# Seven products in place of two projections for two more units, four input sums moved ahead, lambda moved into another scaling

## The chip, the cores and the metric

The kernel runs on one core of one Trainium2 chip. A core has five engines with a queue of instructions each: TensorE (PE, matrix products, with PEld for the load of the stationary operand), VectorE (DVE), ScalarE (ACT), GpSimd (POOL) and SyncE (SP, which here only issues transfers). The engines run side by side and wait for each other through semaphores. The metric is the time of one execution on the device in microseconds, as the median of several runs; lower is better.

## The reference

A sequence of 16 meta tokens and 512 tokens of width 1024 goes through a layer norm and one input projection, whose columns are split into ten blocks of 1024. Two attention branches work on them:

```python
proj = jnp.einsum('bld,dn->bln', h, w_in[i])
q_d, k_d, v_d, g_d, q_s, k_s, v_s, g_s, m_d, m_s = jnp.split(proj, IN_OFFSETS, axis=-1)

# differential attention, 8 heads, two score maps per head
p = jax.nn.softmax(s, axis=-1)
a = p[:, :, 0] - lam * p[:, :, 1]
y_d = jnp.einsum('bhqk,bhkd->bhqd', a, v)

# stick-breaking attention, 16 heads
a = jnp.where(before, jnp.exp(jax.nn.log_sigmoid(z) + suffix), 0.0)
```

`lam` is a scalar made from `diff_lambda`. Both branches are gated with SiLU, projected, merged with sigmoid gates, projected once more, added to the input and normalised.

## The kernel before

**Precision.** Products are made of 32-bit operands split in two: a rounded high part and the remainder. A product of weights and input then takes three matmuls: high by high, high by remainder, remainder by high. A half of a weight tile (128 rows x 512 columns, four blocks of 128) gets its high part by a cast on ACT (`hi`, L183) and its remainder by a subtraction on DVE (`lo`, L188). `prep` does this for the half that lies `ahead` = 4 halves further on than the one being multiplied, and asks for more loads (`fetch`, L144 on SP).

**Units.** The attention is worked in 16 units: eight heads of the differential kind (`d`), then eight pairs of heads of the stick-breaking kind (`s`). The text counts them from one; the code's `u` counts from zero. While unit `u` makes its scores, exponentials, transposes and values, PE also projects the keys and values of unit `u + 1`, the queries of unit `u + 2`, and in some units (`GATE_AT`, from the fifth on) a gate. `run` goes through the projections' generators, which yield estimated times, and puts in the steps of the attention when their time has come; for example `(9.2, store_k)` is placed when 9.2 us of projections, by these estimates, have been emitted. Within the attention part this only gives the priorities: a planner orders each engine's queue by its own estimates when the kernel is built. `placed` ties the first instruction of a step on each engine behind the one emitted before it. The start, and all that comes after the attention, keep the written order.

**Keys and values, first form** (`stage_k`, `stage_v`, `proj_pos`, L510). Two projections of 128 columns each. Each goes over two halves of the 528 positions (264 each) and eight blocks of the 1024 inputs, with three matmuls for each block: 48 matmuls of 264 columns, 96 for both. ACT and DVE split the keys in high part and remainder (L635, L636), and `store_k` sends them to the two key tiles by DMA (L643, L644).

**Keys and values, second form** (`stage_kv`, L690). The two weight tiles and the two halves of the inputs and of the positions make a 2 x 2 by 2 x 2 block product, and the kernel makes it with seven block products in place of eight (Strassen's scheme in Winograd's form). Each is 4 blocks x 3 matmuls of 264 columns, 84 in all. It needs:
- four sums of weight blocks; three are made by DMA, which loads one block and adds others to it in memory (`rawk`, accumulating transfers that POOL issues, L146, four for each unit), one by DVE (L169);
- four sums of input blocks, which all units share. `input_sums(k)` makes a quarter of them: a small copy on POOL (L660), four operations on DVE over 264 columns (L662 to L665), a cast on ACT (L667) and a remainder on DVE (L668) over 1056 columns;
- sums of the products, on ACT and DVE (L701 to L712), and at the end the keys' split (L696, L697) and `store_k`, all at the end of the seven products since the second half of the keys comes out of the last.

`SEVEN` is the first unit (from zero) with the second form. It is 5 here, so the sixth unit's keys and values are the first to be made so, during the fifth unit. The four sets of input sums stand in the first four units, one in each, at step 8.0. The ring of buffers for accumulated weights opens with the third unit.

**The scores of the first kind** (`d_scores`). For each block of 128 queries DVE adds a bias and finds the minimum (L834), ACT takes the exponential and its sum (L838), and DVE joins the two maps: reciprocals of the two sums (L842), the second of them times minus lambda (L843), the first map times its reciprocal (L844), and the second times its own plus the first (L845).

Of the kernel before, what the change touches and what calls it, by code (L numbers as in the profile page):

```python
# [35 lines left out]

ORDERED = [mybir.EngineType.PE, mybir.EngineType.DVE, mybir.EngineType.Activation, mybir.EngineType.Pool]
WARM = 14
SEVEN = 5
TD = [(0.85, 11.0, 14.5), (0.95, 13.0, 16.5)]  # L40
GATE_AT = {4: 0, 5: 1, 6: 2, 7: 3, 8: 4, 11: 5, 14: 6}
LO, HI = slice(0, 64), slice(64, 128)
# [3 lines left out]
def hybrid_block_kernel(ctx: ExitStack, tc: tile.TileContext, x, meta, emb_g, emb_b, w_in, b_gate,  # L46
# [175 lines left out]
    def placed(work, engines=ORDERED):  # L222

        ins = nc.cur_bb.bb.instructions
        n = len(ins)
        work()
        for e in engines:
            new = next((i for i in ins[n:] if i.engine == e), None)
            old = next((ins[m] for m in range(n - 1, max(n - 400, 0), -1) if ins[m].engine == e), None)
            if new is not None and old is not None:  # L230
                follow(new, old)
# [349 lines left out]
    with tc.tile_pool(name="att", bufs=1) as ap:  # L581
# [75 lines left out]
        def input_sums(k):  # L657


            g.tensor_copy(hP[k][:, :, :M], hM[:, k:k + 5:4])  # L660
            b11, b12, b21, b22 = [hP[k][:, m, ts(n, H2)] for m in range(2) for n in range(2)]
            v.tensor_tensor(b22, b12, b22, op=ALU.subtract)  # L662
            v.tensor_tensor(b12, b11, b12, op=ALU.subtract)
            v.tensor_tensor(b11, b22, b11, op=ALU.subtract)
            v.tensor_tensor(b21, b11, b21, op=ALU.add)  # L665
            h, l = tS[0][:, k:k + 5:4], pair_of("tl", F32R)
            s.copy(h, hP[k])  # L667
            v.tensor_tensor(l, hP[k], h.bitcast(F32), op=ALU.subtract)  # L668
            tL.append(l)
# [139 lines left out]
        def d_scores(unit, h):  # L809

            A = unit["A"]


            bias = ap.tile([P, L], F32, tag="bias", name="bias", bufs=2)
            if h == 0:
                g.iota(bias, pattern=[[-1, L]], base=400, channel_multiplier=1, allow_small_or_imprecise_dtypes=True)
                g.affine_select(bias, bias, pattern=[[-1, L]], compare_op=ALU.is_ge, fill=1e30, base=400,
                                channel_multiplier=1)
            g.tensor_scalar(bias, biases[-1] if h else bias, 0.5 if h else -0.5, None, op0=ALU.mult)
            biases.append(bias)  # L820
            a = apads[h % 2]
            mn = ap.tile([P, NB, 2, 2], F32, tag="mn", name="mn", bufs=2)
            zs = ap.tile([P, NB, 2], F32, tag="zs", name="zs", bufs=2)
            rz = ap.tile([P, NB, 2], F32, tag="rz", name="rz", bufs=2)
            for i in reversed(range(NB)):
                nk = NKEY[i]
                e = [E[c][:, ZOFF[i]:ZOFF[i] + nk] for c in range(2)]
                for c in range(2):
                    m = mn[:, i, c, :]
                    for n, (ps, k0, use) in enumerate(logits(A[c], K[c], i)):  # L830
                        if n == 1:
                            yield
                        b0 = 384 - P * i + k0
                        v.tensor_tensor_reduce(e[c][:, k0:k0 + use], ps[:, :use], bias[:, b0:b0 + use], -1.0, 3e38,  # L834
                                               ALU.add, ALU.min, m[:, n:n + 1])
                    if nk > 512:
                        v.tensor_tensor(m[:, 0:1], m[:, 0:1], m[:, 1:2], op=ALU.min)
                    s.activation(e[c], e[c], AF.Exp, scale=-1.0, bias=m[:, 0:1], accum_out=zs[:, i, c:c + 1])  # L838
                    if c == 0:
                        yield  # L840
                r = rz[:, i, :]
                v.reciprocal(r, zs[:, i, :])  # L842
                v.tensor_scalar(r[:, 1:2], r[:, 1:2], nlam, None, op0=ALU.mult)  # L843
                v.tensor_scalar(e[0], e[0], r[:, 0:1], None, op0=ALU.mult)  # L844
                v.scalar_tensor_tensor(a[:, AOFF[i]:AOFF[i] + nk], e[1], r[:, 1:2], e[0], op0=ALU.mult, op1=ALU.add)  # L845
                yield

        def d_values(unit, ta):
# [105 lines left out]
        for u, (kind, n) in enumerate(UNITS):  # L954
            unit = units[u]
            if u + 3 == SEVEN:
                pools["rawk"] = ap
            last = u + 1 == len(UNITS)
            proj = [] if last else keys_values(units[u + 1], *UNITS[u + 1])
            if u + 2 < len(UNITS):  # L960
                proj.append(stage_q(units[u + 2], *UNITS[u + 2]))
            steps = pending + [(0.6, lambda unit=unit: values(unit, kind))]
            pending = []
            if u + 1 < SEVEN:
                steps.append((9.2, store_k))
            if u in range(SEVEN - 5, SEVEN - 1):
                if not tS:
                    tS.append(ypool.tile([P, KT, L], F32R, tag="ys", name="tS"))
                steps.append((8.0, lambda k=u + 5 - SEVEN: placed(lambda: input_sums(k))))
            if u in GATE_AT and u < 14:  # L970
                proj.append(raw_gate(GATE_AT[u], kept["r"][GATE_AT[u]]))
            if kind == "d":
                ta = {}
                dt, t0, t1 = TD[u in GATE_AT]
                steps += spread(d_scores(unit, n), 0.0, dt, 10)
                parts = transposed(ta, apads[n % 2])
                steps += [(t0 + 0.7 * m, f) for m, f in enumerate(parts)]
                steps.append((t1, lambda: d_values(unit, ta)))
                pending = [(3.0 if n < 7 else 5.8, lambda unit=unit, n=n: d_norm(unit, n))]
            else:  # L980
                if n == 0:
                    diag.append(ap.tile([P, L], F32, tag="bias", name="diag", bufs=2))
                    g.memset(diag[0], 0.0)
                    g.tensor_copy(diag[0][:, L - P:], ident)
                    g.memset(v3[:, 1], 0.0)
                    for a in apads:
                        for i in range(NB):
                            g.memset(a[:, ds(AOFF[i] + NKEY[i] - 1, 1)], 0.0)
                if last:
                    ydT = [pair_of("ydT", n=S) for k in range(4)]  # L990
                    ydT = [ydT[k % 4][:, k // 4, :] for k in range(8)]
                    ysT = ypool.tile([P, 8, S], F32, tag="ys", name="ysT")
                    ysT = [ysT[:, k, :] for k in range(8)]
                    unit["y"] = ysT[7]

                    def fill_in(y, of):
                        placed(lambda: nc.sync.dma_start(y, of), [mybir.EngineType.SP])

                    fill_in(ydT[7], kept["d"][7])
                    for m, (y, of) in enumerate(((ydT, "gd"), (ysT, "gs"))):  # L1000
                        for j in range(7):
                            steps.append((1.3 + 1.5 * (7 * m + j), lambda o=y[j], x=kept[of][j]: fill_in(o, x)))
                    proj += [gate("d", n, lambda: ydT[7]), merge_gate(0, 0), merge_gate(0, 1), merge_gate(0, 2),
                             gate("s", n, lambda: ysT[7])]
                else:
                    if GATE_AT.get(u) == n:
                        yd = gpool.tile([P, S], F32, tag="sg", name="yd")
                        nc.sync.dma_start(yd, kept["d"][n])
                        proj.append(gate("d", n, lambda yd=yd: yd, kept["gd"][n]))
                    else:  # L1010
                        steps += zip((12.0, 24.0), late_gate(ap, *(kept[x][n] for x in ("d", "r", "gd"))))
                    proj.append(gate("s", n, lambda unit=unit: unit["y"], kept["gs"][n]))
                for c in range(2):
                    ta = {}
                    steps += spread(s_scores(unit, c, n == 0), (2.0 + 4.3 * c) if n == 0 else 4.4 * c, 0.85, 5)
                    parts = transposed(ta, apads[c])
                    times = LAST[c] if last else [7.0 + 6.5 * c + 0.7 * m for m in range(3)] + [10.5 + 6.5 * c]
                    steps += zip(times, parts)
                    steps.append((times[3], lambda c=c, ta=ta: s_values(unit, c, n, ta)))
                if last:  # L1020
                    steps.append((LAST[0][0] - 0.1, lambda: state.update(ends=len(nc.cur_bb.bb.instructions))))
            run(proj, steps)
# [236 lines left out]
```

## Time and profile before

| | |
|---|---|
| median of 3 runs | 712.65 us (712.34 to 713.63) |
| the profiled execution | 712.22 us, of which the span is 710.4 us |
| PE busy | 697.5 us (98%) |
| weight loads busy (PEld) | 636.9 us (90%) |
| DVE busy | 571.8 us (80%) |
| ACT busy | 439.2 us (62%) |
| POOL busy | 125.6 us (18%) |
| DMA | 123.36 MB, mean 174 GB/s |

The profile is that of one execution. Its rows give for each instruction or group the engine, the line of the kernel, what is written and from what, and a duration. The busy time of an engine counts a moment once, even where two instructions overlap. Matmuls are pipelined: one lasts longer than the distance to the next, so that its price on PE is the distance between starts. A row of waits reads "engine and line that waited <- engine and line that released it: us in total, times, longest".

### The profile page before, as it was taken

What the parts mean: (1) busy time and instruction counts of PE and PEld (TensorE: products, weight loads), DVE (VectorE), ACT (ScalarE), POOL (GpSimd) and SP (SyncE); (2) the same over time, 40 slices, a digit from 0 to 9 for tenths busy, and PEclk for the clock granted to TensorE, in tenths of its full rate; (3) what the DMA queues carried; (4) which work ended last, traced back from release to release, by engine and by line L of the source; (5) the groups of instructions that cost most, each with busy time, mean ns of one, the idle gap of its engine ahead of it and who ended that gap; (6) DMA issues with size and microseconds to landing.
All of it is one profiled execution on the core that took longest, in us unless ns stands there. A gap on an engine that the chain in (4) does not pass through costs nothing.

```text
span 710.4 us, 13389 instructions
## 1 busy us (share of the span) xinstructions
PE 697.5 (98%) x4494; PEld 636.9 (90%) x4494; DVE 571.8 (80%) x1265; ACT 439.2 (62%) x1065; POOL 125.6 (18%) x143
## 2 busy tenths in 40 slices
PE   9999999999999999999999999999999999999994
PEld 8999999989999898988989998988889998999884
DVE  6888897878787777988878889976666788788897
ACT  5766676757667587776857777666455546455300
POOL 3214210212222111212123120000012102220002
PEclk9999999999999999999999999999999999999997
DMA  9368754879888876899897976646576748795902
GB/s 293 93 169 164 167 133 125 184 181 183 198 200 184 201 177 164 186 215 214 200 217 174 206 171 175 166 133 197 178 174 112 164 123 182 133 198 170 322 15 104
DMA packets 182182, 123.36 MB, mean 174 GB/s; under 512 B 9009, under 2 KB 165074, under 8 KB 182114
## 3 DMA queue, kind: packets, MB, share of 16 engines
q1 hardware_dynamic: 148130, 102.32, 50.1%
q0 software_dynamic: 33664, 19.14, 21.6%
q10 hardware_dynamic: 320, 1.06, 0.4%
q8 instruction: 35, 0.57, 0.3%
q14 instruction: 33, 0.27, 0.1%
HBM read 91.96 MB, written 9.44 MB: 143 GB/s over the span
## 4 chain that ended last, share of the span: by engine, by line
PE 86%; DVE 6%; DMA 3%; ACT 2%; issue 1%; POOL 1%; SPq 0%; ACTq 0%; DVEq 0%; POOLq 0%
PE q L690 16%; PE ps L496 12%; PE ps L494 12%; PE ps L495 12%; PE q L1065 10%; PE ps L510 7%; PE sc L754 6%; PE t L766 4%; DMA lgb<-in_ln_b_dram 1%; PE bank L385 1%; PE tv L723 1%; DVE hr L1215 1%; DMA xt<-in_x_dram 1%; PE av L922 1%; DMA raw<-in_w_out_dram 1%
## 5 line engine op out<-in xcount | busy, mean ns | idle before, releaser
L188 DVE TENSOR_TENSOR wl<-raw,wh 128x512 fp32r<-128x512 f32 x169 | 115.7, 691 | 43.7 <-ACT wh L183 42.2
L494 PE MATMUL ps<-hTh,wh 128*128 128x512 f32 x368 | 145.0, 394 | 0.0
L495 PE MATMUL ps<-hTl,wh 128*128 128x512 f32 x368 | 144.5, 393 | 0.0
L496 PE MATMUL ps<-hTh,wl 128*128 128x512 f32 x368 | 144.4, 392 | 0.0
L183 ACT CAST wh<-raw 128x512 fp32r<-128x512 f32 x169 | 104.4, 625 | 28.0 <-PE ps L495 15.3
L496 PEld LDWEIGHTS ps<-hTh,wl 128*128 128x128 f32 x368 | 69.2, 188 | 13.9
L495 PEld LDWEIGHTS ps<-hTl,wh 128*128 128x128 f32 x368 | 69.2, 188 | 13.1
L494 PEld LDWEIGHTS ps<-hTh,wh 128*128 128x128 f32 x368 | 69.2, 188 | 12.9
L146 POOL DMA_DIRECT2D rawk<-in_w_in_dram x44 | 60.8, 1642 | 96.9 <-DMA rawk<-in_w_in_dram 58.4
L754 PE MATMUL sc<-k,A 128*128 128x264 f32 (+3 forms) x320 | 65.9, 299 | 0.1
L1065 PE MATMUL q<-gh,wh 128*128 128x256 f32 x224 | 63.5, 283 | 0.2 <-ACT t L1074 0.2
L1065 PE MATMUL q<-gl,wh 128*128 128x256 f32 x224 | 63.4, 283 | 0.0
L1065 PE MATMUL q<-gh,wl 128*128 128x256 f32 x224 | 63.4, 283 | 0.0
L907 DVE TENSOR_TENSOR_SCAN e<-e,diag 128x528 f32<-128x528 f32 (+1 forms) x64 | 53.4, 848 | 7.5 <-ACT e L901 7.3
L754 PEld LDWEIGHTS sc<-k,A 128*128 128x128 f32 x320 | 50.3, 189 | 3.3 <-ACT e L901 0.3
L690 PE MATMUL q<-tS,wh 128*128 128x264 f32 x176 | 50.9, 290 | 0.9 <-DVE low L612 0.9
L690 PE MATMUL q<-tl,wh 128*128 128x264 f32 x176 | 50.2, 286 | 0.0
L690 PE MATMUL q<-tS,wl 128*128 128x264 f32 x176 | 50.2, 286 | 0.0
L510 PE MATMUL ps<-hTh,wh 128*128 128x264 f32 x160 | 46.4, 290 | 0.2 <-ACT k L632 0.2
L933 POOL DMA_DIRECT2D ys<-half x14 | 11.8, 840 | 195.9 <-ACT ys L932 119.2
L510 PE MATMUL ps<-hTh,wl 128*128 128x264 f32 x160 | 45.6, 286 | 0.0
L510 PE MATMUL ps<-hTl,wh 128*128 128x264 f32 x160 | 45.5, 285 | 0.0
(291 smaller groups left out, 1851.4 us busy)
## 6 DMA issues: line engine op xcount, KB each, us to landing
raw<-in_w_in_dram SPq DMA_DIRECT2D x141, 256.0 KB, 3.3
rawk<-in_w_in_dram POOLq DMA_DIRECT2D x44, 256.0 KB, 6.0
rawk<-in_w_in_dram SPq DMA_DIRECT2D x33, 256.0 KB, 3.9
k<-ks SPq DMA_DIRECT2D x60, 132.0 KB, 3.1
raw<-in_w_out_dram SPq DMA_DIRECT2D x16, 256.0 KB, 3.9
k<-ks SPq DMA_DIRECT2D x60, 66.0 KB, 2.8
A<-low SPq DMA_DIRECT2D x28, 128.0 KB, 2.8
raw<-in_w_br_diff_dram SPq DMA_DIRECT2D x12, 256.0 KB, 4.7
```

Source lines behind the costliest of these rows:

```text
L146: second[l] = [lambda raw=raw, x=x: g.dma_start(raw, x, accum_op=ALU.add) for x in more]
L183: s.copy(wh, raw)
L188: eng.tensor_tensor(wl, raw, wh.bitcast(F32), op=ALU.subtract)
L494: pe.matmul(ps, wh[:, k % 4, :], hTh[:, k, M:], start=(k == 0), stop=False)
L495: pe.matmul(ps, wh[:, k % 4, :], hTl[:, k, M:], start=False, stop=False)
L496: pe.matmul(ps, wl[:, k % 4, :], hTh[:, k, M:], start=False, stop=(k == KT - 1))
L510: pe.matmul(ps[:, :H2], a[:, k % 4, :], b[:, k, ts(c, H2)], start=(k == 0 and m == 0), stop=(k == KT - 1 and m == 2))
L690: pe.matmul(bank, a[:, k, :], b, start=start and k == 0 and j == 0, stop=k == 3 and j == 2, skip_group_check=not start)
L754: pe.matmul(ps[:, :n], q, K[:, m, k0:k0 + n], start=(m == 0), stop=(m == 1))
L766: pe.transpose(t[:, o:o + P], a[:, AOFF[i] + j * P:AOFF[i] + (j + 1) * P], ident)
L907: v.tensor_tensor_scan(rev, rev, diag[0][:, L - nk:][:, ::-1], 0.0, ALU.mult, ALU.max)
L1065: pe.matmul(bank, a[:, k, :], b[:, n, k, :], start=start and k == 0 and m == 0, stop=k == 3 and m == 2, skip_group_check=not start)
```

## The change

Three edits.

1. `SEVEN` becomes 3: the keys and values of the fourth and fifth unit, made during the third and the fourth, take the second form too. Their `store_k` at step 9.2 goes, since `stage_kv` stores by itself; the ring for accumulated weights opens with the first unit in place of the third; and the list of loads has seven weight halves for each of these units where it had four.
2. The four sets of input sums stand in the first unit (three, at steps 5.0, 9.0 and 13.0) and in the second (one, at 5.0).
3. In `d_scores`, minus lambda is multiplied in the scaling of the second map, which now comes first, and the first map is scaled in the operation that joins them. The separate product of one column goes.

```diff
-SEVEN = 5
+SEVEN = 3
...
                 r = rz[:, i, :]
                 v.reciprocal(r, zs[:, i, :])
-                v.tensor_scalar(r[:, 1:2], r[:, 1:2], nlam, None, op0=ALU.mult)
-                v.tensor_scalar(e[0], e[0], r[:, 0:1], None, op0=ALU.mult)
-                v.scalar_tensor_tensor(a[:, AOFF[i]:AOFF[i] + nk], e[1], r[:, 1:2], e[0], op0=ALU.mult, op1=ALU.add)
+                v.tensor_scalar(e[1], e[1], r[:, 1:2], nlam, op0=ALU.mult, op1=ALU.mult)
+                v.scalar_tensor_tensor(a[:, AOFF[i]:AOFF[i] + nk], e[0], r[:, 0:1], e[1], op0=ALU.mult, op1=ALU.add)
                 yield
...
             if u + 1 < SEVEN:
                 steps.append((9.2, store_k))
-            if u in range(SEVEN - 5, SEVEN - 1):
+            if u + 1 < SEVEN:
                 if not tS:
                     tS.append(ypool.tile([P, KT, L], F32R, tag="ys", name="tS"))
-                steps.append((8.0, lambda k=u + 5 - SEVEN: placed(lambda: input_sums(k))))
+                steps += [(5.0 + 4.0 * (k % 3), lambda k=k: placed(lambda: input_sums(k))) for k in range(4) if k // 3 == u]
```

## The prediction

> Units are counted from one: the profile's first unit is the loop's u = 0. Each unit's matmuls start with the keys and values of the unit after it.
>
> **What bounds the kernel now.** I read the page's engine totals first, then a table of stretches cut at the first key matmul of each unit (units one to five), then the chain of waits, then who waits for whom.
>
> ```profile
> PE 697.5 (98%) x4494; PEld 636.9 (90%) x4494; DVE 571.8 (80%) x1265; ACT 439.2 (62%) x1065; POOL 125.6 (18%) x143
> ```
>
> ```profile
> core 0: us, PE busy (x) PEld busy (x) DVE busy (x) ACT busy (x) POOL busy (x), PEclk, DMA share, GB/s
> 39.90:59.50 19.60, 19.60 (x142) 18.58 (x141) 17.91 (x55) 13.19 (x37) 4.41 (x5) 1.00 0.61 165
> 59.50:83.50 24.00, 24.00 (x172) 22.82 (x171) 19.97 (x61) 15.97 (x42) 7.46 (x7) 1.00 0.83 159
> 83.50:107.60 24.10, 24.10 (x173) 22.84 (x173) 20.31 (x61) 16.39 (x43) 3.11 (x2) 1.00 0.76 167
> 107.60:131.70 24.10, 24.10 (x173) 22.87 (x172) 20.73 (x62) 16.41 (x43) 3.13 (x2) 1.00 0.56 141
> 131.70:159.80 28.10, 28.10 (x185) 25.83 (x184) 22.83 (x66) 18.95 (x49) 5.51 (x4) 1.00 0.78 177
> ```
>
> PE has no idle time in the units that change, at a granted clock of 1.00: a matmul taken away there ends the kernel earlier by its interval, as long as PE's operands keep coming. The fifth unit already uses seven products, and is longer only by the gate projection that it carries. In the chain of waits:
>
> ```profile
> 97.50 3.03 PE ps L510 x25
> 409.30 2.92 PE q L690 x24
> ```
>
> A matmul over 264 columns takes 3.03 / 25 = 0.121 us, in the two-projection form (L510), and 2.92 / 24 = 0.122 in the seven-product form (L690). The busy time of one (286 ns) is no price, since they overlap. Outside its start PE waits for another engine almost nowhere:
>
> ```profile
> PE q L690 <- DVE low L612: 0.9, 2, 0.6
> ```
>
> DVE is the engine behind. In the first unit it is busy 17.91 of 19.60 us. What it waits for from the first unit to the fourth (39.9 to 131.7 us), longest first:
>
> ```profile
> DVE wl L188 <- ACT wh L183: 5.6, 4, 2.0
> DVE rz L842 <- ACT e L838: 1.8, 2, 0.9
> DVE ax L788 <- PE t L766: 1.7, 3, 0.8
> DVE am L792 <- ACT am L790: 1.0, 2, 0.5
> DVE ks L636 <- ACT ks L635: 0.5, 1, 0.5
> DVE e L834 <- PE sc L754: 0.3, 1, 0.3
> DVE al L772 <- ACT ah L771: 0.3, 1, 0.3
> ```
>
> That is 11.2 us in four units; the first has 0.8 of it (the rows of L636 and L834), the others 10.4, or 3.5 each. This is the room into which the change can put DVE work.
>
> **The change, part by part.** *Matmuls.* In the third and fourth unit, 96 matmuls of 264 columns (two projections, 2 halves x 8 blocks x 3 terms each) become 84 (7 x 4 x 3). 12 fewer in each, 24 x 0.121 = 2.9 us. The table gives the same another way. The gate of the fifth unit is 24 matmuls of 512 columns, here such a run and what follows it:
>
> ```profile
> 154.32 0.40 PE L494 MATMUL ps<-hTh,wh 128*128 128x512 f32 x1
> 159.79 0.28 PE L690 MATMUL q<-hTh,wh 128*128 128x264 f32 x1
> ```
>
> 24 of them lie between the two starts, 5.47 us. 28.10 - 5.47 = 22.63, against 24.10 of the fourth unit: 1.47 less, twice 2.9.
>
> *DVE.* Prices are from start to start, because ends overlap:
>
> ```profile
> 41.53 1.89 DVE L188 TENSOR_TENSOR wl<-raw,wh 128x512 fp32r<-128x512 f32 x3
> 90.82 0.21 DVE L843 TENSOR_SCALAR rz<-rz,nlam 128x1 f32<-128x1 f32 x1
> 90.95 0.57 DVE L844 TENSOR_SCALAR e<-e,rz 128x528 f32<-128x528 f32 x1
> 97.43 0.42 DVE L665 TENSOR_TENSOR hF<-hF 128x264 f32<-128x264 f32 x1
> 97.78 0.42 DVE L834 CUSTOM_DVE_ANT_0 e<-sc,bias 128x272 f32<-128x272 f32 x1
> 100.12 1.26 DVE L668 TENSOR_TENSOR tl<-hF,tS 128x1056 fp32r<-128x1056 f32 x1
> 101.30 0.30 DVE L834 CUSTOM_DVE_ANT_0 e<-sc,bias 128x144 f32<-128x144 f32 x1
> ```
>
> 512 columns cost (1.89 - 0.69) / 2 = 0.60, 264 columns 0.35, a whole remainder of the sums 1.18, the small lambda product 0.13.
> - A unit that turns to seven products adds three weight remainders and one sum of weights (4 x 0.60) and three more operations over 264 columns (five in place of two): 3.45 us. Two units: 6.9.
> - Lambda: the 0.13 goes, four times a unit. The new first scaling reads two scalars per row in place of one; no row has this pair on these shapes. Bounds: nothing, or another 0.13 (the price of a whole extra operation). I take nothing, because the multiplication adds no pass over the columns: -0.5 in each of the eight units of that kind.
> - One set of input sums is 4 x 0.35 + 1.18 = 2.6. None is added: the first unit gets two more (+5.2), the second keeps one, third and fourth lose theirs.
>
> With each moved set go a copy on POOL (L660) and a cast on ACT (L667) into the first unit, ahead of what those queues held there; POOL is busy 4.41 and ACT 13.19 of its 19.60 us, so they find room.
>
> First unit: +5.2 - 0.5 = +4.7 into 0.8 of room, so DVE is up to 3.9 us late at its end. Second: 3.5 of room and 0.5 freed, which takes up that 3.9. Third and fourth: 3.45 - 2.6 - 0.5 = +0.4, and 1.45 less time, into 3.5: 1.7 left in each. The work fits over four units, but not inside the first.
>
> What becomes late is the weights' remainder (L188), which PE's projections read, and the rows of scores. The weights have cover:
>
> ```profile
> 46.72 0.68 DVE L188 TENSOR_TENSOR wl<-raw,wh 128x512 fp32r<-128x512 f32 x1
> 59.74 0.28 PE L510 MATMUL ps<-hTh,wl 128*128 128x264 f32 x1
> ```
>
> The first is the remainder of the first half of the third unit's key weights, the second its first use: 12.3 us of lead. 3.9 fits in that. Scores that come late let projections go ahead of them, because the engines' order around them is written at build. So the price of the moved sums lies between 0 and 3.9; I take 0.3, near the end that the lead points to.
>
> *ACT.* Three more weight casts and one more copy in the third and fourth unit, less one cast of a sum:
>
> ```profile
> L183 ACT CAST wh<-raw 128x512 fp32r<-128x512 f32 x169 | 104.4, 625 | 28.0 <-PE ps L495 15.3
> ```
>
> Four at 0.63 at most are 2.5, on 16.4 of busy time in 22.6 us. Nothing.
>
> *Transfers.* Each of the two units needs six loads from SP in place of four, and four accumulating ones from POOL. Most of SP's time ahead of a load goes to buffers that are not free:
>
> ```profile
> SPq L144 <- DVE wl L188: 175.7, 77, 7.1
> ```
>
> The loads are early then, not short of bandwidth; the units with seven products and a DMA share of 0.78 have PE busy throughout. Nothing, with the same 12 us of lead as cover.
>
> *Keys.* In the two-projection form the keys are done before the values, and stored at step 9.2. With seven products the second half of the keys comes out of the last one. In the fifth unit:
>
> ```profile
> 148.01 0.28 PE L690 MATMUL q<-hTh,wl 128*128 128x264 f32 x1
> 150.22 0.42 DVE L697 TENSOR_TENSOR ks<-q,ks 128x264 fp32r<-128x264 f32 x1
> 154.69 0.60 SPq L644 DMA_DIRECT2D k<-ks  x1
> 160.16 0.29 PE L754 MATMUL sc<-k,A 128*128 128x264 f32 x1
> k<-ks SPq DMA_DIRECT2D x60, 66.0 KB, 2.8
> ```
>
> From the last product at 148.01 to the landing of the last key store (154.69 + 2.8 = 157.5) pass 9.5 us, and the next scores start at 160.16, 2.7 later. The third and fourth unit have no gate behind the products: the scores would come 5.47 earlier, 2.8 ahead of the keys. PE loses nothing if products of the next unit (84 wait there) stand first in its queue, and 2 x 2.8 = 5.6 if the scores do. I take 0.4, near nothing, because the last store was issued 4.5 us after the remainder that it carries (150.22) with nobody waiting for it, and can come earlier. Behind a store that waits for its keys SP holds weight loads, which are then late by as much; they have the lead above.
>
> *POOL beside DVE.* Eight more accumulating issues. POOL and DVE work at the same time here:
>
> ```profile
> 55.09 1.65 POOL L819 TENSOR_SCALAR bias<-bias 128x528 f32<-128x528 f32 x1 [17.60 <-DVE mn L834]
> 58.23 4.07 POOL L146 DMA_DIRECT2D rawk<-in_w_in_dram  x3
> 55.27 1.68 DVE L668 TENSOR_TENSOR tl<-hF,tS 128x1056 fp32r<-128x1056 f32 x1
> 60.12 0.69 DVE L188 TENSOR_TENSOR wl<-raw,wh 128x512 fp32r<-128x512 f32 x1 [1.16 <-ACT wh L183]
> ```
>
> Beside POOL's arithmetic a remainder of the sums took 1.68 us, where the one at 100.12 took 1.26; beside an accumulating issue the remainder of a weight took its usual 0.69. So the issues cost DVE nothing. [...]
>
> *Sum.* The profiled execution took 712.22 us (span 710.4). -2.9 + 0.3 + 0.4 = -2.2: 710.0. The median of the three runs, 712.65, lies 0.43 above the profiled one, which would make it 710.4. I predict the middle, 710.2.
>
> **The rivals.** *Late keys (slower).* Place: the starts of the fourth and fifth unit. PE's queue has the scores first, both times the full 2.8: 712.2 - 2.9 + 5.6 = 714.9, from the point on where more than 2.9 of it is waited out. For it: the 2.8 above. Against it: the 84 products. At half of it 712.1, no change.
> *The first unit by DVE.* The 3.9 is not carried into the second unit, because scores, exponentials and transposes of one head hang together: 712.2 - 2.9 + 3.9 = 713.2, no change. For it: 17.91 of 19.60 busy. Against it: the 12.3 us of lead.
> *The order elsewhere.* Lambda changes all eight units of the first kind, and so the order at build. The 0.9 that PE waits for L612 could go, or come a second time: 709.3 or 711.1, inside the forecast.
> [...]
>
> **How the numbers follow.** Forecast 0.62, by itself from 708.7 to 711.8; late keys in full 0.10, at half 0.09; the first unit by DVE 0.15; POOL's issues 0.02; something not seen 0.02. About 0.2%, 1.4 us, is what a measurement tells from no change. Of the forecast 0.56 lies below 711.2 and 0.06 above it. With the half-late keys and most of the first unit's rival, no change has 0.26; slower has 0.18, the late keys, the upper part of the DVE rival, POOL and the unseen. The range 708.0 to 714.5 leaves out the fully late keys and what lies beyond, and a gain that is larger than all 24 matmuls and the 0.9 with a little over.
>
> **What would show it.** Right: 288 matmuls on L510 and 1092 on L690's line; the third and fourth unit 22.6 us long; DVE without pauses in the first two units, PE without. Wrong: PE idle ahead of the score products at the start of the fourth or fifth unit (keys), ahead of projections or transposes in the first two (DVE), or a weight remainder beside accumulating issues well over 0.69 us.

## The result, and the profile after

| | median | lowest to highest | ratio to before, 95% interval |
|---|---|---|---|
| before | 712.36 us (10 runs) | 711.76 to 713.63 | |
| after | 716.49 us (10 runs) | 713.99 to 719.24 | 1.0057 [1.0041, 1.0073] |

The change makes the kernel 4.1 us slower. The forecast was 710.2 us; the result lies above the range (708.0 to 714.5). The profiled execution of after took 719.24 us (span 717.4) and is the longest of its ten, so the sizes below are upper ones. That of before took 712.22.

Engine totals of after, and the stretches of the first five units, cut as in the prediction:

```profile
PE 697.0 (97%) x4470; PEld 635.2 (89%) x4470; DVE 578.0 (81%) x1247; ACT 443.9 (62%) x1073; POOL 136.1 (19%) x151
```

```profile
core 0: us, PE busy (x) PEld busy (x) DVE busy (x) ACT busy (x) POOL busy (x), PEclk, DMA share, GB/s
40.10:59.80 19.70, 19.70 (x142) 18.68 (x141) 19.45 (x55) 14.56 (x38) 9.36 (x8) 1.00 1.18 215
59.80:87.70 27.90, 25.85 (x173) 24.40 (x172) 23.13 (x63) 16.19 (x41) 3.14 (x2) 0.94 0.52 120
87.70:110.10 22.40, 22.40 (x159) 21.10 (x158) 21.10 (x58) 16.46 (x46) 5.47 (x5) 1.00 0.85 175
110.10:133.20 23.10, 23.10 (x162) 21.70 (x161) 19.99 (x59) 17.21 (x46) 7.84 (x6) 1.00 0.93 199
133.20:163.00 29.80, 28.55 (x185) 25.97 (x184) 24.01 (x66) 20.41 (x54) 6.00 (x6) 1.00 0.92 201
```

The 24 matmuls are gone (4470 for 4494), and the third unit is 1.7 us shorter (22.40 for 24.10), the fourth 1.0. But the second is 3.9 longer (27.90 for 24.00), though PE's work in it is the same, and the fifth 1.7 (29.80 for 28.10). In the second PE is idle for 2.05 us and its granted clock is 0.94. Who PE waits for, in the whole of after (total, times, longest):

```profile
PE sc L754 <- DMA k<-ks: 5.0, 4, 2.1
PE q L690 <- DVE low L612: 0.8, 2, 0.6
PE av L916 <- ACT af L802: 0.8, 1, 0.8
```

The first row is new: by this view the score products wait for `store_k`'s transfers, 5.0 us in four places. Three of them, in the order of time on PE:

```profile
62.34 0.88 PE L754 MATMUL sc<-k,A 128*128 128x264 f32 x4 [2.05 <-DMA k<-ks]
...
136.51 0.49 PE L754 MATMUL sc<-k,A 128*128 128x264 f32 x2 [1.25 <-DMA k<-ks]
...
346.39 0.85 PE L754 MATMUL sc<-k,A 128*128 128x264 f32 x4 [1.48 <-DMA k<-ks]
```

The wait at 62.34 ends 0.1 us after the landing of the key store that the row names (issued at 56.68, 5.5 us to land), and so does the one at 346.39 (issued at 343.41, by its semaphore landed at 346.25). The one at 136.51 doesn't. The view puts a wait down to the semaphore that moved last, and the key stores issued just before it were still under way. SP's rows, and the landings in the views of tile `A` for the transfer issued at 131.91 and of tile `k` for the two at 133.99:

```profile
130.86 1.67 SPq L614 DMA_DIRECT2D A<-low  x2
...
DMA to landing us min/median/max: 4.5/4.5/4.5
...
133.99 1.28 SPq L643 DMA_DIRECT2D k<-ks  x2
...
DMA to landing us min/median/max: 3.8/4.0/4.1
```

The two key stores land at 137.8 and later, after the scores have started. What lands 0.1 us ahead of them, at 131.91 + 4.5 = 136.4, is the remainder of the queries (`low`, L614). So 1.25 of the 5.0 us belong to the queries.

**A ledger** of the two profiled executions, 7.0 us apart: the third and fourth unit -2.7; the second +3.9; the fifth +1.7; twelfth to fourteenth +3.8 (2.0, 1.4 and 0.4, units of the second kind, which the change doesn't touch). The remaining 0.3 is spread.

**The second unit's keys.** They are made in the first unit, still by two projections. On DVE (L636), SP (L643, L644) and PE of before:

```profile
49.64 0.42 DVE L636 TENSOR_TENSOR ks<-ps,ks 128x264 fp32r<-128x264 f32 x1
...
48.58 0.55 SPq L644 DMA_DIRECT2D k<-ks  x1
50.14 1.33 SPq L643 DMA_DIRECT2D k<-ks  x2
...
54.02 1.32 SPq L643 DMA_DIRECT2D k<-ks  x2
55.40 0.60 SPq L644 DMA_DIRECT2D k<-ks  x1
...
59.87 0.65 PE L754 MATMUL sc<-k,A 128*128 128x264 f32 x4
```

And of after:

```profile
50.01 0.43 DVE L636 TENSOR_TENSOR ks<-ps,ks 128x264 fp32r<-128x264 f32 x1
...
48.95 1.72 SPq L644 DMA_DIRECT2D k<-ks  x1
50.77 0.95 SPq L144 DMA_DIRECT2D raw<-in_w_in_dram  x1
51.82 2.86 SPq L643 DMA_DIRECT2D k<-ks  x2
...
56.68 1.58 SPq L643 DMA_DIRECT2D k<-ks  x2
58.31 0.64 SPq L644 DMA_DIRECT2D k<-ks  x1
```

DVE is 0.4 us later with the last remainder, but SP is 2.9 later with the last store. Its first issues take longer (1.72 for 0.55 us, 2.86 for 1.33; the rows don't tell why), and then, from 53 to 60 us, its waits name something new, the landing of earlier weight loads:

```profile
SPq L643 <- DMA raw<-in_w_in_dram: 0.7, 2, 0.4
```

Such loads took 3.3 us to land in this stretch (33 to 60 us, median) and now take 8.9; the store at 56.68 leaves 0.1 us after the landing of the one issued at 44.98. The landings of the key stores, in the view of the tile `k`, before and then after:

```profile
DMA to landing us min/median/max: 1.9/2.1/2.4
```

```profile
DMA to landing us min/median/max: 4.4/5.1/9.0
```

The first scores don't need the last store: in after they start at 62.34, before it lands (58.31 + 4.7 = 63.0). They need the one at 56.68. Before, the same one left at 54.02 and was there 2.4 us later, at 56.4, 3.5 us ahead of the scores at 59.87. Now it leaves 2.7 later and takes 3.1 longer, 5.8 together, 2.3 beyond that; the pause is 2.05. What is new beside these transfers is on POOL. Before, its first accumulating transfer stood behind the stores:

```profile
56.69 1.52 POOL L146 DMA_DIRECT2D rawk<-in_w_in_dram  x1
```

In after they begin 20 us earlier:

```profile
36.03 1.52 POOL L146 DMA_DIRECT2D rawk<-in_w_in_dram  x1
...
38.10 3.68 POOL L146 DMA_DIRECT2D rawk<-in_w_in_dram  x2
...
43.06 2.96 POOL L146 DMA_DIRECT2D rawk<-in_w_in_dram  x2
```

The DMA share in the first unit is 1.18, where it was 0.61 (it adds up the time of all packets, so that it can pass 1).

### The profile page after: what moved, and what is told of

Its sections match the earlier page's. It is cut to its first block, busy times and chain, and to the rows that moved or that the text cites. A ratio compares the mean times of both kernels' runs of the same rounds, so it can differ in the third digit from the quotient of the medians.

```text
span 717.4 us, 13367 instructions
## 1 busy us (share of the span) xinstructions
PE 697.0 (97%) x4470; PEld 635.2 (89%) x4470; DVE 578.0 (81%) x1247; ACT 443.9 (62%) x1073; POOL 136.1 (19%) x151
## 4 chain that ended last, share of the span: by engine, by line
PE 85%; DMA 5%; DVE 5%; ACT 3%; issue 1%; POOL 1%; SPq 0%; DVEq 0%; ACTq 0%; POOLq 0%
PE q L690 18%; PE ps L495 12%; PE ps L494 12%; PE ps L496 12%; PE q L1064 10%; PE sc L754 6%; PE ps L510 4%; PE t L766 3%; DMA k<-ks 2%; DMA raw<-in_w_out_dram 2%; PE bank L385 1%; PE tv L723 1%; DMA xt<-in_x_dram 1%; DVE hr L1214 1%; DMA eb<-in_emb_ln_b_dram 1%
## 5 line engine op out<-in xcount | busy, mean ns | idle before, releaser
L183 ACT CAST wh<-raw 128x512 fp32r<-128x512 f32 x167 | 102.9, 625 | 35.2 <-PE ps L495 19.5
L146 POOL DMA_DIRECT2D rawk<-in_w_in_dram x52 | 71.8, 1628 | 126.5 <-DMA rawk<-in_w_in_dram 67.0
L754 PE MATMUL sc<-k,A 128*128 128x264 f32 (+3 forms) x320 | 67.6, 301 | 5.8 <-DMA k<-ks 5.0
L690 PE MATMUL q<-tS,wh 128*128 128x264 f32 x208 | 60.5, 291 | 0.8 <-DVE low L612 0.8
L690 PE MATMUL q<-tl,wh 128*128 128x264 f32 x208 | 59.4, 286 | 0.0
L690 PE MATMUL q<-tS,wl 128*128 128x264 f32 x208 | 59.3, 286 | 0.0
L771 ACT CAST ah<-t 128x512 fp32r<-128x512 f32 (+2 forms) x72 | 34.3, 478 | 18.6 <-PE t L766 18.2
L690 PE MATMUL q<-hTh,wh 128*128 128x264 f32 x156 | 45.4, 291 | 0.0
L188 DVE TENSOR_TENSOR wl<-rawk,wh 128x512 fp32r<-128x512 f32 x52 | 35.6, 684 | 11.6 <-ACT wh L183 11.6
```

The lines of the kernel that those rows point to most:

```text
L146: second[l] = [lambda raw=raw, x=x: g.dma_start(raw, x, accum_op=ALU.add) for x in more]
L183: s.copy(wh, raw)
L188: eng.tensor_tensor(wl, raw, wh.bitcast(F32), op=ALU.subtract)
L690: pe.matmul(bank, a[:, k, :], b, start=start and k == 0 and j == 0, stop=k == 3 and j == 2, skip_group_check=not start)
L754: pe.matmul(ps[:, :n], q, K[:, m, k0:k0 + n], start=(m == 0), stop=(m == 1))
L771: s.copy(h, t[:, o:o + w])
```

## The experiments

Each is timed against the kernel before on the same chip; the ratio has its 95% interval. Two theories stood at the start: the early accumulating transfers delay the key stores; or DVE, with three sets of sums in the first unit, and the order built around lambda do it.

**Three parts alone, on the kernel before.** The sums moved:

```diff
-            if u in range(SEVEN - 5, SEVEN - 1):
+            if u < 2:
...
-                steps.append((8.0, lambda k=u + 5 - SEVEN: placed(lambda: input_sums(k))))
+                steps += [(5.0 + 4.0 * (k % 3), lambda k=k: placed(lambda: input_sums(k))) for k in range(4) if k // 3 == u]
```

> The kernel before, with the four sets of input sums where the change has them (three in the first unit, one in the second), nothing else. Theory 'DVE': the first unit's DVE is late by up to 3.9 us, PE pauses in the first or second unit, the time 714 to 716. Theory 'transfers': DVE's work is taken up by the pauses of the second unit, key stores land as before, no PE pause over 0.3 us in the first two units, 712.4 within 1 us.

The two scalings with lambda, as in the change:

```diff
-                v.tensor_scalar(r[:, 1:2], r[:, 1:2], nlam, None, op0=ALU.mult)
-                v.tensor_scalar(e[0], e[0], r[:, 0:1], None, op0=ALU.mult)
+                v.tensor_scalar(e[1], e[1], r[:, 1:2], nlam, op0=ALU.mult, op1=ALU.mult)
```

> The kernel before, with lambda inside the second scaling, nothing else. By the prediction's own sum: 0.5 us of DVE less in each of the first eight units, none of it on the path, 712.4 within 1 us. Theory 'order' (any edit in the scores reorders all queues at build, and the stick-breaking units pay for it): PE's pauses from the ninth unit on change by 1 to 4 us in total, up or down, and the time with them, 711 to 716.

The ring for accumulated weights open from the first unit:

```diff
-            if u + 3 == SEVEN:
+            if u == 0:
                 pools["rawk"] = ap
```

> The kernel before, with one edit: the ring of buffers for accumulated weights opens with the first unit in place of the third. Keys and values stay in the first form for the third and fourth unit, sums and lambda stay as before. Theory 'transfers' (the accumulating loads that come early fill the DMA engines in the first unit, so that the key stores of the second unit land late and PE pauses ahead of its scores): PE waits for key stores about 2 us at the start of the second unit, the granted clock falls behind it, key stores land in about 5 us in place of 2.1, the second unit is some 4 us longer than 24.0, the time 714 to 717. Theory 'DVE' (the input sums in the first unit make it late): no sums are moved here, so no pause and 712.4 within 1 us.

Measured: 712.13 us, 0.9995 [0.9985, 1.0005]; 712.00, 0.9998 [0.9989, 1.0007]; and 712.79, 1.0011 [0.9996, 1.0025] (of the last one's ten runs one took 3956 us, from a cause not known; the median doesn't move by it). No part costs anything measurable alone. DVE falls as the cause: with the sums moved PE has no new pause in the first units. The early ring shows more. Its stores land as slowly, and its last one leaves at 57.05, but PE's only wait for key stores is 0.4 us, and that is in the twelfth unit, at 341.66; in the second there is none. The view of its tile `k`:

```profile
DMA to landing us min/median/max: 4.6/6.1/7.9
```

The store that the first scores need leaves at 55.37 and lands at 60.0, and they start at 60.15. Early transfers use up the 3.5 us that it had; they don't overdraw it in every order.

**The eight accumulating transfers of the fourth and fifth unit's weights taken out of after.** Their weight sums are incomplete. PE, DVE, ACT and SP keep after's order, instruction for instruction.

```diff
+    LEFT_OUT = [l for l, x in enumerate(loads) if x[2] == "rawk"][:6]
...
                     second[l] = [lambda raw=raw, x=x: g.dma_start(raw, x, accum_op=ALU.add) for x in more]
+                    if l in LEFT_OUT:
+                        second[l] = []
```

> The changed kernel without the eight accumulating transfers of the fourth and fifth unit's weights: their three plain loads into the ring stay, the blocks that would be added to them are left out, so that these two units' keys and values come from incomplete weight sums. Matmuls, DVE and ACT work are the same. Theory 'transfers': with 2 MB less on the DMA engines the key stores of the second unit land in 3 us or less, the pause of 2.2 us ahead of its scores and the fall of the clock go; the time 711 to 713.5 in place of 716.5. Theory 'keys come late by their place alone' (last product, no gate behind): the pause at the second unit, whose keys are of the first form, is no matter of it; a pause of 1 to 2 us at the fourth or fifth unit stays. Theory 'order': the same pauses as the changed kernel has, 715 to 717.5.

712.92 us, 1.0015 [1.0000, 1.0029]: 3.6 less than after. Landings, the last store and the first two units in this kernel's trace:

```profile
DMA to landing us min/median/max: 1.9/2.1/2.4
```

```profile
55.07 0.61 SPq L647 DMA_DIRECT2D k<-ks  x1
```

```profile
39.70:59.30 19.60, 19.60 (x142) 18.58 (x141) 18.75 (x55) 14.20 (x38) 1.84 (x1) 1.00 0.65 178
59.30:83.40 24.10, 24.10 (x173) 22.84 (x172) 22.39 (x63) 16.23 (x41) 1.84 (x1) 1.00 0.38 97
```

The stores are as early and as quick as before, with DVE as busy as the change makes it, and the second unit has its 24.1 us again. The fifth has 28.2. So in after's order these transfers cause both pauses, and the fall of the clock behind the first. The two traces exaggerate this: after's is the longest of its ten executions, this one (711.89) the shortest. And 712.92 is still no gain: the twelfth unit, for one, is 39.7 us long, where it was 38.0, with a wait of 1.36 us for a key store at 339.32.

**The old lambda back in after.**

```diff
-                v.tensor_scalar(e[1], e[1], r[:, 1:2], nlam, op0=ALU.mult, op1=ALU.mult)
+                v.tensor_scalar(r[:, 1:2], r[:, 1:2], nlam, None, op0=ALU.mult)
+                v.tensor_scalar(e[0], e[0], r[:, 0:1], None, op0=ALU.mult)
```

> The changed kernel with lambda as it was (its own product of one column, the first map scaled first); seven products from the fourth unit and the moved sums stay. Theory 'transfers': the pause of about 2 us ahead of the second unit's scores stays, with the fall of the clock; third and fourth unit 22.5 us each; 713 to 717. Theory 'order': the pauses of the stick-breaking units go back to those of before (about 4 us of excess in place of 7.6), which makes it 2 to 4 us faster than the changed kernel.

713.57 us, 1.0010 [0.9996, 1.0025]: 2.9 less than after, though lambda alone is worth nothing. The early transfers are the same, the last store leaves at 57.01, and PE's second unit has no pause; neither have the units of the second kind. In their place there is one at the start of the fourth unit (in this trace, the second shortest of its ten, 711.82 us):

```profile
PE sc L754 <- DMA A<-low: 1.9, 1, 1.9
```

That is the place of the prediction's late keys, but the row names the queries. Their remainder leaves SP behind the unit's last key store and lands at 106.62 + 4.5 = 111.1, 0.1 us ahead of the scores. The key store lands at 105.32 + 4.5 = 109.8; PE stood from 109.35 on, so the keys alone would have cost 0.6. What lambda changes is the order of the whole attention, and with it which transfer has too little room.

**A gate behind the products for the fourth and fifth unit.** Gates are moved so that the third and fourth unit carry one, whose 24 matmuls (5.47 us) stand between the last product and the next scores, while the ninth and twelfth lose theirs; with the old lambda, with the new one, and on the kernel before:

```diff
-GATE_AT = {4: 0, 5: 1, 6: 2, 7: 3, 8: 4, 11: 5, 14: 6}
+GATE_AT = {2: 0, 3: 1, 4: 2, 5: 3, 6: 4, 7: 5, 14: 6}
```

> The changed kernel with lambda as before, and the six raw gate projections that stood in the fifth to the ninth and the twelfth unit standing in the third to the eighth: each unit that makes its successor's keys with seven products has a gate (24 matmuls of 512 columns, 5.5 us of PE) behind them. Theory 'late stores' (key and query stores land after the next unit's first scores because only the query projection lies between): the pause of 2.0 us at the start of the fourth unit goes, no new one at the fifth to eighth; the 24 matmuls saved show, 709 to 711.5 in place of 713.6. Rival 'crowded DMA' (the transfers are slow wherever the scores stand): pauses stay, 712 to 715.

> The changed kernel (lambda inside the second scaling) with the same move of the six gates to the third to eighth unit. Theory 'late stores': the pause at the fifth unit goes; the one at the second unit, where keys are of the first form and no gate was added ahead, stays: 712 to 716. If both orders (this and the one with lambda as before) come out alike, lambda's part is the order at build and not its work.

> The kernel before with the six gates moved to the third to eighth unit and nothing else: sums, lambda and seven products from the sixth unit on stay. It separates the two parts of the kernel with early gates (0.9965 of before). Theory 'late stores' (the gates only hide the stores of units that newly have seven products; the gain is that of 24 matmuls): 712 within 1 us. Rival (the gates themselves fill PE better in the first eight units): 709.5 to 711.5.

With the old lambda 709.87 us (six runs), 0.9965 [0.9953, 0.9976], 2.5 faster than before; with the new one 713.34, 1.0016 [1.0005, 1.0026]; on the kernel before 714.24, 1.0036 [1.0021, 1.0050]. The gate takes away the fourth unit's pause, and it isn't the move's own gain: alone it costs 1.9, with a wait of 1.75 us for a key store at 317.68. The new lambda costs 3.5 here, again by key stores, now in units of the second kind:

```profile
PE sc L754 <- DMA k<-ks: 2.7, 2, 1.5
```

**Only one more unit with seven products**, with the old lambda.

```diff
-SEVEN = 3
+SEVEN = 4
```

> The changed kernel with lambda as before and seven products from the fifth unit on in place of the fourth: one unit more than before, the ring of accumulated weights opens with the second unit, sums as in the change. Twelve matmuls are saved, 1.45 us: 711.0 if no store is late. Theory 'late stores': the fifth unit's keys, made in the fourth without a gate, are late by about 2 us at the fifth unit: 712.5 to 713.5. Theory 'transfers' (the crowd in the first unit is what costs): the ring opens later, key stores of the second unit land as before, no pause over 0.5 us: 710.5 to 711.5.

713.18 us, 1.0008 [0.9998, 1.0018]. Half of the saving, 12 matmuls, doesn't show either: PE waits 2.1 us for key stores, 1.7 of them at one place, 342 us. The time is the one that 'late stores' gave, but not the place: at the start of the fifth unit there is no pause, although no gate stands ahead of it.

**The ring opened at step 4.0 of the first unit**, on the kernel with early gates and old lambda.

```diff
-            if u + 3 == SEVEN:
-                pools["rawk"] = ap
...
+            if u == 0:
+                steps.append((4.0, lambda: pools.update(rawk=ap)))
```

> The kernel with early gates and lambda as before, with the ring of accumulated weights opening at step 4.0 of the first unit in place of its start, so that the plain loads into it and the accumulating ones come some 5 us later. Theory 'transfers': fewer of them stand beside the key stores of the second unit, which land in 3 to 4 us in place of 4.3, and the pause of 1.4 us at the second unit shrinks below 1: 708.5 to 709.6 in place of 709.9. If the loads only move along to the same place: 709.9 within 0.7.

709.15 us (five runs), 0.9958 [0.9943, 0.9974]: the fastest, 3.2 below before. From 39 to 300 us PE waits for nothing; the kernel without this edit had a pause of 1.3 for key stores in the second unit. But not because the transfers start later: POOL issues its first at 35.91 and the landings' median is 5.3. SP issues the last store at 55.69, where it was 57.82. Between the two kernels, 0.7 us is less than their intervals tell apart.

**A small shift in the order of after**: the sums at steps 5.6, 9.6 and 13.6.

```diff
-                steps += [(5.0 + 4.0 * (k % 3), lambda k=k: placed(lambda: input_sums(k))) for k in range(4) if k // 3 == u]
+                steps += [(5.6 + 4.0 * (k % 3), lambda k=k: placed(lambda: input_sums(k))) for k in range(4) if k // 3 == u]
```

> The changed kernel with the three sums of the first unit at steps 5.6, 9.6 and 13.6 in place of 5.0, 9.0 and 13.0 (and the fourth at 5.6): the same instructions, a slightly other order at build. Theory 'order' (where the scores stand in the queue against the late stores is what costs, and it is set by chance of the planner): the time moves by more than 1 us from 716.5, most likely down, 713 to 715.5. Theory 'lambda's work' (the second scaling itself costs): 716.5 within 0.7.

714.87 us, 1.0030 [1.0017, 1.0044]. PE's order differs from after's in some ten places. The second unit's pause is gone, and one of 2.6 us stands at 342 us, again for key stores. The same work, in orders that differ by a little, pauses at other places.

**The transfers taken out of two more kernels.** The eight, out of the one with the old lambda; and all 52 of the keys' and values' weights out of after. Both leave weight sums incomplete.

```diff
-    LEFT_OUT = [l for l, x in enumerate(loads) if x[2] == "rawk"][:6]
+    LEFT_OUT = [l for l, x in enumerate(loads) if x[2] == "rawk"][:99]
```

> The changed kernel with lambda as before (713.6), without the eight accumulating transfers of the fourth and fifth unit's weights, as in the earlier run of that kind; the weight sums of these two units stay incomplete, all other work is the same. Here no pause stood in the stick-breaking units, only one of 2.0 us ahead of the fourth unit's scores. Theory 'transfers are all of it in this order': that pause goes and the prediction's sum comes out, 709.5 to 710.8. Theory 'order or DVE holds a rest': 711.5 to 713.

> The changed kernel without any accumulating transfer of key and value weights (52 of them; the weight sums of thirteen units are incomplete), all other work as in it. Theory 'transfers' for the stick-breaking units too: their key stores land sooner, the pauses at the tenth to fourteenth unit (7.5 us of excess in the ninth to fifteenth unit together) shrink to 4 or less, 709 to 710.5. Theory 'one key tile' (stores can't start before the previous unit's last scores, which stand late in this order): the pause of 1.5 us at the twelfth unit stays at 1 us or more, 711 to 713.

The first: 711.62 us, 0.9989 [0.9971, 1.0006]. Its pause at the fourth unit stays:

```profile
111.61 0.72 PE L757 MATMUL sc<-k,A 128*128 128x264 f32 x4 [2.37 <-DMA A<-A]
```

Here too it is the queries' remainder (105.67 + 5.8 = 111.5); the `A<-A` of the row lands at 113.0 only. So these eight transfers aren't its cause; a gate behind the products removes it, as shown above. The median is 2.0 below that of the old lambda with the transfers, about as much as the intervals can tell, and the two traces don't show where. The second: 711.29 us, 0.9983 [0.9969, 0.9997], 1.6 below the kernel without the eight, and the twelfth unit's pause is gone:

```profile
PE av L919 <- ACT af L805: 0.8, 1, 0.8
PE sc L757 <- DMA k<-ks: 0.2, 1, 0.2
```

There too the transfers took part, and the theory of one key tile falls. It still isn't 709.5, the matmuls' full worth below 712.36. Where the rest is, these runs don't settle: two pauses of 0.8 and 0.7 us remain in units of the second kind, behind ACT and DVE.

## Why the prediction was wrong, step by step

- **Matmuls, -2.9: right.** 24 fewer; the third unit is 22.4 us long, the fourth 23.1, and its sum said 22.63. The gain can be had: the two kernels with early gates and old lambda are 2.5 and 3.2 below before.
- **Sums on DVE, late by up to 3.9, priced 0.3: right.** Of the work put into the first unit a part slides into the second: with the sums moved alone DVE is busy 0.8 us more in the first (18.75 of 19.60) and 3.0 more in the second, and the time stays. In after the keys' remainder is 0.4 late. The rival *first unit by DVE* falls. Lambda's part was taken too large: alone it frees 3.0 us of DVE in the eight units, not 4, since a scaling with two scalars took 550 to 560 ns over 528 columns in six of after's eight rows (760 and 890 in the others), where one with a single scalar took 495 in the mean in before. Nothing hangs on that.
- **ACT: right.** At most it is busy 17.21 of 23.10 us in the units that change, and PE doesn't wait for it there.
- **POOL beside DVE: right.** The remainders of all weights, with 71.8 us of accumulating issues beside them, last as long in the mean as before (691 ns), the accumulated ones among them (684 for 685). No run shows that an accumulating issue holds DVE up, which the prediction gave 0.02.

```profile
L188 DVE TENSOR_TENSOR wl<-raw,wh 128x512 fp32r<-128x512 f32 x167 | 114.6, 691 | 36.4 <-ACT wh L183 32.3
...
L146 POOL DMA_DIRECT2D rawk<-in_w_in_dram x52 | 71.8, 1628 | 126.5 <-DMA rawk<-in_w_in_dram 67.0
...
L188 DVE TENSOR_TENSOR wl<-rawk,wh 128x512 fp32r<-128x512 f32 x52 | 35.6, 684 | 11.6 <-ACT wh L183 11.6
```

- **Transfers, "Nothing, with the same 12 us of lead as cover": wrong, and the largest miss.** The loads did have that lead: PE doesn't wait for weights there. The step asked only whether the weights come in time. It didn't ask what else is under way at that moment: key stores of which the critical one had 3.5 us to spare, and an SP that waits for the landing of loads before it issues them (0.7 us from 53 to 60 us in after). The run without the eight transfers prices this at 3.6 us in after's order.
- **Keys, "0 to 5.6, I take 0.4": wrong in the choice and in the transfer, right in the bounds.** PE pauses for 1.25 us at the fifth unit in after, and for 1.9 at the fourth with the old lambda. Both times the queries' remainder lands last, which the prediction doesn't price at all; the keys alone would have cost nothing in the first case and 0.6 in the second. The rival *late keys* named the place and the cover that is missing, and with gates there the pause goes; that it named them is luck as far as the keys go. The cover isn't missing in every order: without a gate, the kernel with one more unit and the one without the eight transfers have no pause there. The argument for taking the low end, that a store issued 4.5 us late with nobody waiting could come earlier, was wrong: in after the last one is again issued 4.5 us after its remainder (134.66 for 130.18), behind the queries and other stores on SP. And the landing was taken as a constant (2.8), though in the first unit it was 5.1 beside the early transfers and 2.1 without them. Why the queries' remainder is late wasn't tested.
- **The order elsewhere, 0.9 either way: wrong in size.** Lambda's operations cost nothing (712.00 alone), but with them the time is 2.9 us longer in the changed kernel and 3.5 with early gates. That it is the order the planner builds around them, and not their work, is argued from this; the small shift of the sums, which moves the order and no work, is worth 1.6. The order decides whether a key store meets its scores in units as late as the twelfth. The rows of SP in after show how little room there is, first the store, then what such stores waited for between 333 and 346 us:

```profile
343.41 1.29 SPq L643 DMA_DIRECT2D k<-ks  x2
...
SPq L643 <- DMA rawk<-in_w_in_dram: 1.0, 1, 1.0
```

 and the store and the scores of before:

```profile
336.56 1.28 SPq L643 DMA_DIRECT2D k<-ks  x2
...
340.01 0.41 PE L754 MATMUL sc<-k,A 128*128 128x264 f32 x2
```

 Before, the store left 3.5 us ahead of the next scores. In after it leaves 0.4 us after the landing of a weight load that took 7.8 us (issued at 335.20), lands at 346.2, and the scores start at 346.39. Without all 52 transfers, in the same order on PE, that wait isn't there; the store leaves 2.8 us ahead of its scores (335.20 and 337.97), and the pause is gone.

Of the signs that the prediction gave, the one on keys came (PE idle ahead of the scores of the fifth unit), though by the queries, and "PE without pauses in the first two units" failed, by a mechanism that no rival had.

## What to carry to other kernels

When a change starts transfers earlier, list every small transfer that someone waits for within the new stretch (here keys and queries), with its spare time (issue and landing against first use), not only the lead of the loads that move. Check by the landings which transfer a wait was for: where several are under way, the name in a row of waits can be that of another. An operation that costs nothing by itself can still move the time by microseconds where a planner orders the queues at build: compare the orders before crediting or blaming an edit. Where a change takes away the work that stood between a store and its use, put other work there; with the old lambda the same seven products gave nothing without a gate behind them (713.57), and 2.5 us with one.

## What the runs showed of the hardware that was not expected

**The clock after a short pause.** In after the granted clock changes at 62.75, 66.16 and 711.28 us, whole multiples of 3.413 us apart. Cut at such times, the stretch of after that holds its first pause, and the next:

```profile
59.34:62.75 3.41, 1.36 (x9) 1.09 (x8) 3.06 (x4) 1.42 (x4) 0.00 (x0) 1.00 1.12 255
62.75:66.16 3.41, 3.41 (x18) 3.41 (x17) 0.79 (x4) 0.29 (x1) 0.00 (x0) 0.50 0.71 205
```

PE is idle for 2.05 us of the first; then the granted clock is 0.50 for the whole of the second. That is 0.5 x 3.41 = 1.7 us of full clock lost, nearly as much again as the pause: 2.05 + 1.7 of the 3.9 by which this unit is longer. The shifted order shows the same around its pause of 2.6 us:

```profile
338.53:341.94 3.41, 1.19 (x10) 0.98 (x8) 1.12 (x2) 1.63 (x4) 0.00 (x0) 1.00 0.55 142
341.94:345.36 3.42, 3.06 (x12) 3.08 (x13) 1.26 (x1) 1.56 (x4) 0.00 (x0) 0.50 0.89 247
```

But the pause of 2.37 us in the kernel with the old lambda and without the eight transfers falls across two stretches of this length, and the clock stays at 1.00:

```profile
106.60:110.02 3.42, 2.64 (x20) 2.33 (x18) 1.35 (x3) 2.55 (x7) 0.00 (x0) 1.00 1.10 203
110.02:113.43 3.41, 1.82 (x15) 1.86 (x16) 1.20 (x5) 1.17 (x3) 0.54 (x1) 1.00 0.91 201
113.43:116.85 3.42, 3.42 (x30) 3.38 (x29) 3.42 (x13) 2.59 (x8) 2.06 (x2) 1.00 0.73 133
```

So in these traces the length of a pause alone doesn't decide: behind 2.05 and 2.6 us the clock was 0.50, behind 2.37 it stayed at 1.00. In these few it goes with how long PE is busy within one stretch: behind one with 1.36 and one with 1.19 us the next ran at 0.50; behind one with 1.82, and one with 2.16 in the changed kernel (134.43 to 137.84 us), at 1.00. What happens between 1.36 and 1.82 no run shows.

**Landing of small stores.** In the first unit a key store took 2.1 us to land in the median before, 5.1 in after, beside accumulating transfers (9.0 at most), and 2.1 again without the eight of them. Over the whole execution the stores of 66 KB took 2.8 in the median, in before and in after alike.

**The spread.** After's ten runs lie 5.3 us apart, before's 1.9, the best kernel's five 1.2. It doesn't simply go with the pauses: the kernel with one more unit waits 2.1 us for key stores and its ten lie 1.7 apart. What makes it wasn't tested.
